# Second feed-forward layer: nine column blocks by seven products, paired PSUM banks, a weight sum on VectorE, whole weight splits

## The chip, the core and the metric

The kernel runs on one core of one Trainium2 chip. The metric is device time in microseconds (us), the median of several executions. TensorE (PE in the profile) multiplies, VectorE (DVE) and ScalarE (ACT) work elementwise, GpSimd (POOL) issues the accumulating DMAs, SyncE (SP) issues the other DMAs. Each engine executes its own instructions in the order in which the built program lists them.

## What is computed

The layer ends in a SwiGLU feed-forward block on 256 tokens of width 2048, and a last normalisation:

```python
def half_step_ffn(x, mod, i, g, w_up, w_down):
    h = adaln(x, g, mod, i)
    a, b = jnp.split(h @ w_up, 2, axis=-1)
    return x + 0.5 * mod[:, i + 2, None, :] * ((jax.nn.silu(a) * b) @ w_down)
...
    xl = half_step_ffn(xl, mod_l, 6, g_norm[l, 2], w_ffn2_up[l], w_ffn2_down[l])
return rms_norm(xl, g_final)
```

`w_up` is 2048 x 11264 and `w_down` 5632 x 2048, in float32. Everything ahead of this second feed-forward block (the first one, attention, the mLSTM heads) is untouched.

## The kernel before

The 5632 hidden columns are 11 blocks of 512, numbered 0 to 10. Block 0 is prepared ahead. For each of the blocks 1 to 10 an **up** step makes the 256 x 512 gated hidden values, which PE transposes (L2052) into `hid2h`/`hid2l`; for each of the blocks 0 to 10 a **down** step multiplies them by 512 rows of `w_down` and adds to `acc2`.

Float32 precision comes from splitting each operand into a high and a low part: `mm3` (L145 to L149) issues three matmuls for each product of a 128 x 128 stationary and a 128 x 512 moving tile. Weights arrive by SP as 128 x 2048 tiles of 1 MB in `raw`, a tile of three buffers. `split` (L117) makes `hi` by ACT (L125) and `lo` by DVE (L126), in two halves of 1024 columns, each in four buffers, so two weight tiles' worth. A `raw` buffer is free again when `hi` and `lo` are made from it; a `hi` or `lo` buffer when PE has read it. These tiles lie in the pool `wp`, which is open for the whole kernel.

An up step comes in two kinds. The **plain** one (`up`, L2151) takes 8 weight tiles and 192 matmuls. The **seven-product** one (`quad`, L2071) regards tokens and inner dimension as 2 x 2 blocks (`a11`, `a12`, `a21`, `a22`) and the weights as 2 x 2 blocks too (first or second half of the inner dimension, gate part a or value part b), and needs seven block products instead of eight: 168 matmuls, with 14 splits of weight tiles, since sums of weight blocks are factors too. Those sums are built in place: `accum` (L728) is a DMA by POOL that adds another weight block to the tile. The table `order` (L2128) gives the seven products in the order `a11, a12, n1, s4, s2, s3, a22`; `n1, s4, s2, s3` are sums of token blocks that `token_forms` makes once. Each product has two weight tiles (q = 0, 1) of 12 matmuls each; X and Y are the PSUM banks that collect them, read by DVE (L2073, L2074) and ACT.

Before the change the blocks 1, 3, 5, 7, 9 go by seven products and 2, 4, 6, 8, 10 by the plain way. A pacing factor, `PACE2`, lays the quads' 70 pieces beside the 73 plain units (an eighth of an up step or a quarter of a down step, one weight tile of 24 matmuls each), so one piece and one unit alternate. Each down unit has its own two PSUM banks, which DVE adds to `acc2` (L2197).

Of the kernel before, what the change touches and what calls it, by code (L numbers as in the profile page):

```python
# [19 lines left out]
P = 128  # L20
# [18 lines left out]
PACE2 = 70 / 73  # L39

# [16 lines left out]
def tile_layer(ctx: ExitStack, tc: tile.TileContext, I: dict, out: bass.AP):  # L57
# [4 lines left out]
    wp = ctx.enter_context(pool(name="wp", bufs=2))  # L62
# [6 lines left out]
    edge.tile([P, 56], F32, name="edge")  # L69

# [46 lines left out]
    def split(raw, n=2048):  # L117

        half = n // 2
# [1806 lines left out]
    with f2x:  # L1926
        def hid_tiles():

            return [f2.tile([P, FB, T], F32R, tag=g, name=g) for g in ("hid2h", "hid2l")]
# [48 lines left out]
        chain_ = [f3.tile([P, 2048], F32, tag=f"c{q}", name=f"chain2{q}") for q in range(2)]  # L1978
# [3 lines left out]
        QUADS = range(1, LAST, 2)  # L1982
# [4 lines left out]
        for q in range(2):  # L1987
            nc.sync.dma_start(chain_[q], part(QUADS[0], 0, q))

# [3 lines left out]
        forms2 = {g: f3.tile([P, 2, 8, P], F32R, tag=f"f{i}", name=f"{g}f") for i, g in enumerate(("n1", "s4", "s2", "s3"))}  # L1993
        n1, s4, s2, s3 = ([x[:, 0], x[:, 1]] for x in (forms2[g] for g in ("n1", "s4", "s2", "s3")))

        def ra_tile():
            return f2b.tile([P, 2048], F32, tag="ra", name="ra")

        def token_forms():
# [3 lines left out]
            f32 = lambda x: [y.bitcast(F32) for y in x]  # L2003

# [16 lines left out]
            v = ra_tile()[:, :1024].rearrange("p (k c) -> p k c", k=8)  # L2021
# [9 lines left out]
            v = ra_tile()[:, :1024].rearrange("p (k c) -> p k c", k=8)  # L2031
# [6 lines left out]
        summed = set()  # L2038

        def turned():  # L2040

            if not turn:
                return
            n, t, sa, sign = turn[0]
            if n >= 2 and n - 2 not in summed or n - 1 not in hids or (n - 1, 0) in [x[:2] for x in turn] or (n - 1, 1) in [x[:2] for x in turn]:
                return
# [17 lines left out]
        def wait_turn(n, t, sa, sign):  # L2064
            turn.append((n, t, sa, sign))
            turn.sort(key=lambda x: x[:2])

# [3 lines left out]
        def quad(n):  # L2071
# [3 lines left out]
            B, ra, g = {}, {}, {}  # L2075
# [17 lines left out]
            def c12():  # L2093
                add(g["b"], B["X"], g["b"])
                mul(g["a"], g["a"], g["b"])
                wait_turn(n, 0, g["a"], -1.0)
# [7 lines left out]
            def c21():  # L2104
# [3 lines left out]
                wait_turn(n, 1, g["a"], -1.0)  # L2108
# [4 lines left out]
            def again(q):  # L2113
                if n + 2 in QUADS:
                    nc.sync.dma_start(chain_[q], part(n + 2, 0, q))

            def loaded(q):
                ra[q] = ra_tile()
                nc.sync.dma_start(ra[q], part(n, 1, 2 + q))
                return ra[q]  # L2120

            def plain(q):
# [4 lines left out]
            held = lambda q: chain_[q]  # L2127
            order = (  # L2128
                (a11, held, "X", True, chained(1, 0), p1),
                (a12, plain, "Y", True, None, c11),  # L2130
                (n1, held, "Y", True, chained(1, 2), kept),
                (s4, loaded, "Y", False, lambda q: accum(ra[q], part(n, 1, q)), p35),
                (s2, held, "X", False, chained(0, 2), c12),
                (s3, lambda q: ra[q], "X", False, None, c22),
                (a22, held, "Y", True, again, c21),
# [15 lines left out]
        def up(n):  # L2151

            sab = []
            for ab in range(2):
                bs = [bank() for _ in range(2)]
                for u in range(4):
# [7 lines left out]
                    if u == 3:  # L2164
                        for t in range(2):
                            if ab:
                                nc.vector.tensor_tensor(sab[t], sab[t], bs[t], op=ALU.mult)
                                wait_turn(n, t, sab[t], 1.0)
# [5 lines left out]
        def block(n, wt, t):  # L2174

            b = bank()
            tt = slice(t * P, (t + 1) * P)
            for j in range(FB):
                w = slice(j * CB, (j + 1) * CB)
                mm3(b, hids[n][0][:, j, tt], hids[n][1][:, j, tt], *wt(w), j == 0, j == FB - 1)  # L2180
            return b

        late = {}

        def down(n):

            assert (n, 1) in done or not n
            for cb in range(NCB):
                wt = load_split(I["w_dn2"][n, cb])
                for t in range(2):  # L2190
# [3 lines left out]
                    if n == 0:  # L2194
                        nc.scalar.activation(a, b, AF.Copy)
                    else:
                        nc.vector.tensor_tensor(a, a, b, op=ALU.add)  # L2197
                    if n == LAST - 1:
                        half_gated(a, a, late["g8"][:, c])
                        accum(a, x2d[t * P : (t + 1) * P, c])  # L2200
# [4 lines left out]
        def units():  # L2205
            yield from up(2)
            yield from down(0)
            for n in (4, 6, 8):
                yield from up(n)
                yield from down(n - 3)  # L2210
                yield from down(n - 2)
            yield from down(7)
            yield from up(10)
            yield from down(8)
# [7 lines left out]
        def quads():  # L2222
            for n in QUADS:
                yield from quad(n)

        forms = token_forms()
        side, n_side, n_quads = quads(), 0, 14 * len(QUADS)
        for u, _ in enumerate(units()):
            steps(forms)
            turned()  # L2230
            while n_side < n_quads and n_side < (u + 1) * PACE2:
                next(side)
                n_side += 1
                turned()
        assert n_side == n_quads
# [159 lines left out]
```

## Time and profile before

| | us |
|---|---|
| median of 3 runs | 2618.13 (2616.05 to 2618.64) |
| profiled execution, first to last instruction | 2616.0 |
| PE busy in it | 2593.1 |
| DVE busy | 2099.3 |
| ACT busy | 1393.4 |
| second feed-forward block on PE, first to last 128 x 512 matmul | 1948.65 to 2606.6 |

The span of the profiled execution is within 0.1 us of the fastest run and 2.1 us under the median. The page gives busy time by engine, then the span in 40 slices, the DMA queues, the chain of work that ended last, and the costliest groups of instructions. A group is a line of the kernel, an engine, an operation, and the tiles it writes and reads. The answers of the trace give the same for a stretch of time, and name what ended an engine's idle time.

### The profile page before, as it was taken

What the parts mean: (1) busy time and instruction counts of PE and PEld (TensorE: products, weight loads), DVE (VectorE), ACT (ScalarE), POOL (GpSimd) and SP (SyncE); (2) the same over time, 40 slices, a digit from 0 to 9 for tenths busy, and PEclk for the clock granted to TensorE, in tenths of its full rate; (3) what the DMA queues carried; (4) which work ended last, traced back from release to release, by engine and by line L of the source; (5) the groups of instructions that cost most, each with busy time, mean ns of one, the idle gap of its engine ahead of it and who ended that gap; (6) DMA issues with size and microseconds to landing.
All of it is one profiled execution on the core that took longest, in us unless ns stands there. A gap on an engine that the chain in (4) does not pass through costs nothing.

```text
span 2616.0 us, 33774 instructions
## 1 busy us (share of the span) xinstructions
PE 2593.1 (99%) x12742; PEld 2159.5 (83%) x12742; DVE 2099.3 (80%) x2792; ACT 1393.4 (53%) x1798; POOL 208.8 (8%) x261
## 2 busy tenths in 40 slices
PE   8999999999999999999999999999999999999998
PEld 5788888888888888888889889878898888888887
DVE  7788888878888788888886889788887676767767
ACT  5455444444444565444454367557576655555554
POOL 0000010100010100000110000220000000000001
PEclk9999999999999999999999999999999999999999
DMA  9889999999999988889986877777769897988875
GB/s 399 347 213 267 281 267 281 256 275 276 277 274 281 265 248 236 226 214 229 230 243 262 311 272 253 240 245 270 248 231 299 261 252 253 253 248 257 242 225 175
DMA packets 126932, 678.93 MB, mean 260 GB/s; under 512 B 14120, under 2 KB 16680, under 8 KB 64944
## 3 DMA queue, kind: packets, MB, share of 16 engines
q1 hardware_dynamic: 99408, 499.54, 51.4%
q0 software_dynamic: 27360, 177.22, 34.9%
q8 instruction: 100, 1.64, 0.2%
q14 instruction: 64, 0.52, 0.1%
HBM read 658.82 MB, written 17.89 MB: 259 GB/s over the span
## 4 chain that ended last, share of the span: by engine, by line
PE 92%; DVE 3%; DMA 3%; issue 1%; ACT 1%; POOL 0%; SPq 0%; ACTq 0%; POOLq 0%; DVEq 0%
PE mm L147 24%; PE mm L149 24%; PE mm L148 24%; PE mm L85 2%; PE tr L148 2%; PE tr L149 2%; PE tr L147 2%; PE Y L149 1%; PE Y L148 1%; PE Y L147 1%; DMA mraw<-in_w_m 1%; PE X L147 1%; PE X L149 1%; PE X L148 1%; PE tr L85 1%; DVE lo L126 1%
## 5 line engine op out<-in xcount | busy, mean ns | idle before, releaser
L125 ACT ACTIVATE hi<-raw 128x1024 fp32r<-128x1024 f32 (+3 forms) x536 | 556.5, 1042 | 579.6 <-PE mm L149 448.8
L126 DVE TENSOR_TENSOR lo<-raw,hi 128x1024 fp32r<-128x1024 f32 (+1 forms) x524 | 630.1, 1208 | 288.2 <-ACT hi L125 268.8
L125 ACT ACTIVATE hi<-chain 128x1024 fp32r<-128x1024 f32 x320 | 338.1, 1060 | 257.3 <-PE mm L149 150.1
L126 DVE TENSOR_TENSOR lo<-chain,hi 128x1024 fp32r<-128x1024 f32 x320 | 386.8, 1221 | 84.4 <-ACT hi L125 80.0
L147 PE MATMUL mm<-hi,hhi 128*128 128x512 f32 (+3 forms) x1024 | 394.6, 385 | 0.0
L148 PE MATMUL mm<-lo,hhi 128*128 128x512 f32 (+3 forms) x1024 | 387.6, 379 | 0.0
L149 PE MATMUL mm<-hi,hlo 128*128 128x512 f32 (+3 forms) x1024 | 387.3, 378 | 0.0
L205 DVE SCALAR_TENSOR_TENSOR junk<-sraw,cBh 128x1024 fp8e5<-128x1024 f32 x192 | 234.4, 1221 | 26.0 <-DMA sraw<-in_w_mt 23.7
L149 PEld LDWEIGHTS mm<-hi,hlo 128*128 128x128 f32 x1024 | 192.9, 188 | 34.0
L147 PEld LDWEIGHTS mm<-hi,hhi 128*128 128x128 f32 x1024 | 192.9, 188 | 31.4
L148 PEld LDWEIGHTS mm<-lo,hhi 128*128 128x128 f32 x1024 | 193.2, 189 | 30.7
L149 PE MATMUL mm<-hi,hid2l 128*128 128x512 f32 x352 | 137.4, 390 | 0.0
L147 PE MATMUL mm<-hi,hid2h 128*128 128x512 f32 x352 | 137.2, 390 | 0.0
L148 PE MATMUL mm<-lo,hid2h 128*128 128x512 f32 x352 | 137.1, 389 | 0.0
L148 PE MATMUL mm<-lo,h2hi 128*128 128x512 f32 x320 | 124.9, 390 | 0.1
L147 PE MATMUL mm<-hi,h2hi 128*128 128x512 f32 x320 | 124.9, 390 | 0.0
L149 PE MATMUL mm<-hi,h2lo 128*128 128x512 f32 x320 | 124.6, 389 | 0.0
L205 DVE SCALAR_TENSOR_TENSOR sr<-sr,cBl 128x1024 f32<-128x1024 f32 x85 | 102.8, 1219 | 14.7 <-DMA sr<-in_w_mt 14.4
L728 POOL DMA_DIRECT2D chain<-in_w_up1b x60 | 53.0, 884 | 725.3 <-DVE lo L126 698.4
L147 PE MATMUL mm<-hhi,hi 128*128 128x512 f32 (+1 forms) x288 | 101.2, 351 | 0.0
L149 PE MATMUL mm<-hhi,lo 128*128 128x512 f32 (+1 forms) x288 | 98.9, 343 | 0.0
L148 PE MATMUL mm<-hlo,hi 128*128 128x512 f32 (+1 forms) x288 | 98.9, 343 | 0.0
(514 smaller groups left out, 5456.3 us busy)
## 6 DMA issues: line engine op xcount, KB each, us to landing
raw<-in_w_dn SPq DMA_DIRECT2D x70, 1024.0 KB, 7.0
chain<-in_w_up1b POOLq DMA_DIRECT2D x60, 1024.0 KB, 10.5
raw<-in_w_up2b SPq DMA_DIRECT2D x50, 1024.0 KB, 5.7
sraw<-in_w_mt SPq DMA_DIRECT2D x96, 512.0 KB, 8.7
sr<-in_w_mt SPq DMA_DIRECT2D x82, 512.0 KB, 5.3
raw<-in_w_up1b SPq DMA_DIRECT2D x40, 1024.0 KB, 8.1
mraw<-in_w_m SPq DMA_DIRECT2D x32, 1024.0 KB, 7.6
chain<-in_w_dn POOLq DMA_DIRECT2D x30, 1024.0 KB, 8.6
```

Source lines behind the costliest of these rows:

```text
L85: ins = getattr(self.engine, name)(*a, **k)
L125: scalar[0].activation(hi, src, AF.Copy)
L126: vector[0].tensor_tensor(lo, src, hi.bitcast(F32), op=ALU.subtract)
L147: tensor[0].matmul(out_ap, sh, mh, start=first, stop=False, skip_group_check=skip)
L148: tensor[0].matmul(out_ap, sh, ml, start=False, stop=False, skip_group_check=skip)
L149: tensor[0].matmul(out_ap, sl, mh, start=False, stop=last, skip_group_check=skip)
L205: ins = nc.vector.scalar_tensor_tensor(junk() if junk else raw, raw, 1.0, cB[s], op0=ALU.mult, op1=ALU.mult, accum_out=mT[:, i, s, kt, h : ...
L728: accum = lambda dst, src: nc.gpsimd.dma_start(dst, src, accum_op=ALU.add)
```

## The change

- Blocks 2 to 10 go by seven products, block 1 alone by the plain way. The order is now fixed: three plain units, then the nine quads one after another, with one plain unit after the products `a12`, `n1`, `s2`, `s3` (in the first quad also after the others).
- The down steps of blocks 1 to 8 go in pairs (`down_pair`): two blocks' products collect in the same two banks, and DVE adds to `acc2` once for both.
- The tile of the third weight block, which was loaded a second time and added by an accumulating DMA, is loaded once and early (`next_third`) and added to the chain by DVE, 128 x 2048, after the split of `n1`'s tile. Two sets of two chain tiles, c and r, change roles from quad to quad.
- `wp` moves to the right side and is closed at the start of this block. Its place goes to `f3`, which now holds the weights: `raw` in **two** buffers, `hi` and `lo` whole (128 x 2048) in **three**. `token_forms` takes one of the two `raw` buffers for its intermediate values, and writes `s3` over `a21`.

```diff
 def raw_tile(n=2048):
+    if wide:
+        return wide["pool"].tile([P, 2048], F32, tag="raw", name="raw", bufs=2)
...
 def split(raw, n=2048):
+    if wide:
+        hi, lo = (wide["pool"].tile([P, 2048], F32R, tag=x, name=x, bufs=3) for x in ("hi", "lo"))
+        nc.scalar.activation(hi, raw, AF.Copy)
+        nc.vector.tensor_tensor(lo, raw, hi.bitcast(F32), op=ALU.subtract)
...
+wcm.__exit__(None, None, None)
 f3 = ctx.enter_context(pool(name="f3", bufs=1, side="right"))
-acc2 = f2.tile([P, 2, D], F32, name="acc2", bufs=1)
+wide["pool"] = f3
+acc2 = f3.tile([P, 2, D], F32, name="acc2")
+sets = [[f3.tile([P, 2048], F32, tag=f"{g}{q}", name=f"chain2{g}{q}") for q in range(2)] for g in "cr"]
-QUADS = range(1, LAST, 2)
+QUADS = range(2, LAST + 1)
 for q in range(2):
-    nc.sync.dma_start(chain_[q], part(QUADS[0], 0, q))
+    nc.sync.dma_start(sets[0][q], part(QUADS[0], 0, q))
+for q in range(2):
+    nc.sync.dma_start(sets[1][q], part(QUADS[0], 1, 2 + q))
...
+        raw = raw_tile()
+        vs = [raw[:, x * 1024 : (x + 1) * 1024].rearrange("p (k c) -> p k c", k=8) for x in range(2)]
...
-    (n1, held, "Y", True, chained(1, 2), kept),
-    (s4, loaded, "Y", False, lambda q: accum(ra[q], part(n, 1, q)), p35),
+    (n1, held, "Y", True, lambda q: add(chain_[q], chain_[q], ra[q]), kept),
+    (s4, third, "Y", False, lambda q: accum(ra[q], part(n, 1, q)), p35),
     (s2, held, "X", False, chained(0, 2), c12),
-    (s3, lambda q: ra[q], "X", False, None, c22),
-    (a22, held, "Y", True, again, c21),
+    (s3, third, "X", False, next_first, c22),
+    (a22, held, "Y", True, next_third, c21),
...
+def down_pair(n):
+    bs = {}
+    for c0 in (0, 2):
+        for m in (n, n + 1):
+            for cb in (c0, c0 + 1):
+                if m == n:
+                    bs[cb] = [bank() for _ in range(2)]
+                wt = load_split(I["w_dn2"][m, cb])
+                for t in range(2):
+                    block(m, wt, t, bs[cb][t], m == n, m > n)
+                if m > n:
+                    for t in range(2):
+                        a = acc2[:, t, cb * CB : (cb + 1) * CB]
+                        nc.vector.tensor_tensor(a, a, bs[cb][t], op=ALU.add)
+                yield
...
+for _ in range(3):
+    unit()
     steps(forms)
+for n in QUADS:
+    behind = {0: 2, 1: 1, 2: 1, 3: 1, 4: 1, 5: 1, 6: 1} if n == QUADS[0] else {1: 1, 2: 1, 4: 1, 5: 1}
+    for step, _ in enumerate(quad(n)):
+        if step % 2:
+            unit(behind.get(step // 2, 0))
+        if n == QUADS[0] and step == 7:
+            drain(forms)
```

How the change moves instructions is shown at two places; the lines of the changed kernel count on by some numbers, L147 there is the load in `load_split` (L140 before), L124 is the whole `lo`, L2081 an addition.

**First place: SP's queue where this block begins.** `raw_15956` and `raw_16015` are the last loads of the part ahead. Before, the first three weight tiles of `up(2)` follow, each in a `raw` buffer that DVE has read, and then the chain's two tiles:

```order
L140 DMA raw_15956<-in_w_up2 128x2048 [waits DMAHW7_49,DMAHW4_49,DVE_49]
L140 DMA raw_16015<-in_w_up2 128x2048 [waits DMAHW5_49,DMAHW0_49,DVE_49]
L140 DMA raw_16110<-in_w_up2b 128x2048 [waits DMAHW6_49,DVE_49]
L140 DMA raw_16172<-in_w_up2b 128x2048 [waits DMAHW7_49,DVE_49]
L140 DMA raw_16233<-in_w_up2b 128x2048 [waits DMAHW0_49,DVE_49]
L1988 DMA chain20_16100<-in_w_up2b 128x2048 [waits DVE_49,PE_49]
```

In the changed program:

```order
L147 DMA raw_15956<-in_w_up2 128x2048 [waits DMAHW7_49,DMAHW4_49,DVE_49]
L147 DMA raw_16015<-in_w_up2 128x2048 [waits DMAHW5_49,DMAHW0_49,DVE_49]
L1997 DMA chain2c0_16101<-in_w_up2b 128x2048 [waits DMAHW0_49,DMASW0_49,DMAHW6_49,DVE_49,DMAHW7_49,PE_49,Activation_49]
L1997 DMA chain2c1_16102<-in_w_up2b 128x2048
L1999 DMA chain2r0_16103<-in_w_up2b 128x2048
L1999 DMA chain2r1_16104<-in_w_up2b 128x2048
L147 DMA raw_16114<-in_w_up2b 128x2048
L147 DMA raw_16150<-in_w_up2b 128x2048 [waits DMAHW5_49,DVE_49]
L147 DMA raw_16184<-in_w_up2b 128x2048 [waits DMAHW6_49,DVE_49]
```

Four chain tiles stand ahead of the first `raw`, and the first of them waits for PE: its wait is for the last matmul of the part ahead, which reads the closed pool's `hi` and `lo`. `raw_16150`, `raw_16184` and the seven `raw` loads after them each wait for the `lo` of the `raw` load just before, since `token_forms` holds the other buffer.

**Second place: DVE and SP around the turn from one quad to the next** (here from block 6 to block 7). DVE before, in a quad: whole tiles in two halves, a `raw` unit and a chain piece in turn:

```order
L126 TENSOR_TENSOR lo_17252<-chain20_16100,hi_17251 128x1024
L2073 TENSOR_TENSOR ca_17097<-Y_17135,ca_17097 128x512
L126 TENSOR_TENSOR lo_17256<-chain20_16100,hi_17255 128x1024
L126 TENSOR_TENSOR lo_17275<-raw_17272,hi_17274 128x1024
L126 TENSOR_TENSOR lo_17279<-raw_17272,hi_17278 128x1024
L126 TENSOR_TENSOR lo_17309<-chain21_16101,hi_17308 128x1024
```

DVE in the changed program (the first two rows are `a11`'s tiles, `raw_18027` and `raw_18045` those of `a12`, `raw_18065` is the down unit behind it, `chain2c0` in the ninth row is `n1`'s first tile):

```order
L124 TENSOR_TENSOR lo_17984<-chain2c0_16101,hi_17983 128x2048
L124 TENSOR_TENSOR lo_18008<-chain2c1_16102,hi_18007 128x2048
L2081 TENSOR_TENSOR ca_17910<-Y_17944,ca_17910 128x512
L124 TENSOR_TENSOR lo_18030<-raw_18027,hi_18029 128x2048
L2082 TENSOR_TENSOR ca_17910<-ca_17910,cy_17728 128x512
L124 TENSOR_TENSOR lo_18048<-raw_18045,hi_18047 128x2048
L2069 SCALAR_TENSOR_TENSOR hid2l_17867<-tr_18000,hid2h_17866 128x4x128
L124 TENSOR_TENSOR lo_18068<-raw_18065,hi_18067 128x2048
L2081 TENSOR_TENSOR ca_18024<-Y_18026,ca_18024 128x512
L124 TENSOR_TENSOR lo_18099<-chain2c0_16101,hi_18098 128x2048
L2219 TENSOR_TENSOR acc2_16100<-acc2_16100,mm_17834 128x512
L2081 TENSOR_TENSOR chain2c0_16101<-chain2c0_16101,chain2r0_16103 128x2048
```

And SP there:

```order
L2132 DMA raw_18045<-in_w_up2b 128x2048 [waits DMAHW7_49,DMAHW3_49,DVE_49]
L2128 DMA chain2r0_16103<-in_w_up2b 128x2048 [waits DMASW4_49,DVE_49]
L2128 DMA chain2r1_16104<-in_w_up2b 128x2048 [waits DMASW5_49,DVE_49]
L147 DMA raw_18065<-in_w_dn2 128x2048 [waits DMAHW0_49,DVE_49]
L147 DMA raw_18136<-in_w_dn2 128x2048 [waits DMAHW3_49,DVE_49]
```

Six weight tiles (`a22`'s, `a11`'s, `a12`'s) now follow each other without a unit between them, and `raw_18065` takes the buffer of `raw_18027`: its load waits for `lo_18030`, two splits ahead of its own.

More of the change, by code (lines that the diff above doesn't have):

```diff
@@ L1927, in hid_tiles @@
         def hid_tiles():
-            return [f2.tile([P, FB, T], F32R, tag=g, name=g) for g in ("hid2h", "hid2l")]
+            return [f2.tile([P, FB, T], F32R, tag=g, name=g, bufs=3) for g in ("hid2h", "hid2l")]
         def sab_tile():
@@ L2095, in c12 @@
                 mul(g["a"], g["a"], g["b"])
-                wait_turn(n, 0, g["a"], -1.0)
+                turn.append((clock[0] + 2, n, 0, g["a"], -1.0))
             def c22():
@@ L2172, in up, with block @@
                     yield
-        def block(n, wt, t):
-            b = bank()
+        def block(n, wt, t, b=None, first=True, last=True):
+            b = b if b is not None else bank()
             tt = slice(t * P, (t + 1) * P)
@@ L2205, in units @@
         def units():
[L2206 to L2214, printed above, removed]
+            yield from up(1)
+            yield from down0()
+            for n in range(1, LAST - 2, 2):
+                yield from down_pair(n)
         def before_final():
```

106 lines of the change are left out of this document (55 added, 51 removed).

## The prediction

> **What bounds the kernel now.** I read the page's busy times first, then the stretch of the second feed-forward block, then who waits in it.
>
> ```profile
> span 2616.0 us, 33774 instructions
> PE 2593.1 (99%) x12742; PEld 2159.5 (83%) x12742; DVE 2099.3 (80%) x2792; ACT 1393.4 (53%) x1798; POOL 208.8 (8%) x261
> ...
> 1948.65:2606.60 657.95, 657.84 (x2939) 543.36 (x2937) 479.95 (x485) 368.79 (x393) 42.42 (x49) 1.00 0.84 248
> ...
> ACT hi L125 <- PE mm L149: 196.8, 135, 3.3
> DVE lo L126 <- ACT hi L125: 159.8, 129, 2.8
> ```
>
> The third row is the block alone: its length, then busy time of PE, weight load, DVE, ACT, POOL, the granted clock (1.00), the DMA engines' share (0.84) and GB/s. PE is busy for 657.84 of 657.95 us, DVE for 480 and ACT for 369. The waits agree: ACT waits for PE to free a `hi` buffer, 196.8 us in all, and DVE waits for ACT. So PE sets the time, and everything that reaches it comes early. A busy PE is not yet a PE at its peak, so I take its rate from two matmuls eleven steps apart:
>
> ```profile
> 2603.67 0.39 PE L147 MATMUL mm<-hi,hid2h 128*128 128x512 f32 x1
> ...
> 2606.16 0.39 PE L149 MATMUL mm<-hi,hid2l 128*128 128x512 f32 x1
> ```
>
> 2.49 us by 11 is 0.2264 us each. The block has 5 x 192 (plain up) + 5 x 168 (quads) + 11 x 96 (down) = 2856 such matmuls, 646.6 us; the rest of 657.9 are the transposes. There is no slack to win but in the number of matmuls.
>
> **What the change removes.** Four plain up steps become quads: 4 x (192 - 168) = 96 matmuls, 96 x 0.2264 = **21.7 us** less on PE. That is the whole gain; all other savings are on engines that PE does not wait for. Paired banks drop 32 of 72 additions of 682 ns from DVE, but DVE gets 178 whole splits for 302 halves and 2 whole ones, 18 weight sums and four more quads' six additions:
>
> ```profile
> L126 DVE TENSOR_TENSOR lo<-raw,hi 128x1024 fp32r<-128x1024 f32 x182 | 221.8, 1223 | 151.7 <-ACT hi L125 150.8
> L126 DVE TENSOR_TENSOR lo<-chain,hi 128x1024 fp32r<-128x1024 f32 x80 | 97.0, 1221 | 8.8 <-ACT hi L125 5.8
> L2197 DVE TENSOR_TENSOR acc<-acc,mm 128x512 f32<-128x512 f32 x72 | 49.1, 682 | 4.7 <-PE mm L149 4.6
> L126 DVE TENSOR_TENSOR lo<-ra,hi 128x1024 fp32r<-128x1024 f32 x40 | 48.7, 1222 | 5.1 <-ACT hi L125 3.2
> L2254 DVE TENSOR_TENSOR lo<-raw,hi 128x2048 fp32r<-128x2048 f32 x2 | 4.6, 2283 | 0.0
> L2253 ACT ACTIVATE hi<-raw 128x2048 fp32r<-128x2048 f32 x2 | 3.8, 1920 | 1.4 <-DMA raw<-in_w_dn 1.4
> ```
>
> 178 x 2.28 = 406 against 372 us now; 18 sums at the price of a whole `lo`, 2.28 (no sum of this shape runs today; its nearest row is the same operation on the same sizes) are 41; 24 additions are 16; 32 fall, 22. DVE rises from 480 to about 545 of some 636 us. On average it still fits, so I charge nothing for DVE's total; where it stands in the way locally comes below. Six accumulating DMAs for each quad instead of eight, on POOL, free DMA time, but four more quads use it up.
>
> **What it adds, first place: the opening.** Today the block's first weights are on the way long before PE wants them:
>
> ```profile
> 1931.56 10.46 SPq L140 DMA_DIRECT2D raw<-in_w_up2b  x3
> ...
> L149 PE MATMUL tr<-h2hi,lo x32: 281/283/283, 1937.5 to 1948.7; 128*128 128x256 f32 x32
> ...
> L147 PE MATMUL mm<-hi,h2hi x320: 388/389/486, 1948.8 to 2536.3; 128*128 128x512 f32 x160
> ```
>
> Three loads start from 1931.6, and PE goes over from the part ahead (last matmul at 1948.7) without a gap. In the changed program SP's first load waits for that last matmul, its end at about 1949, and four chain tiles go ahead of the first `raw`. How fast five loads land, and one alone, and one beside accumulates, three stretches show:
>
> ```profile
> DMA packets 3197, 21.24 MB, mean 425 GB/s; under 512 B 352, under 2 KB 352, under 8 KB 992
> ...
> raw<-in_w_up2b SPq DMA_DIRECT2D x3, 1024.0 KB, 4.8
> ...
> raw<-in_w_dn SPq DMA_DIRECT2D x6, 1024.0 KB, 7.6
> chain<-in_w_up2b POOLq DMA_DIRECT2D x3, 1024.0 KB, 10.5
> ```
>
> The first row is a stretch of plain loads alone (10 to 60 us), the second 2152 to 2186 us, without accumulates, the others 2104 to 2148 us, with them. Five tiles are 5.24 MB: 12.3 us at 425 GB/s, and 2.2 more, since one tile of 2.5 us at that rate takes 4.8. So `raw` lands 14.5 us after PE stopped; `hi` takes 1.92, `lo` 2.28, with handovers 0.2: PE starts in earnest after **18.9 us**.
>
> Then one `raw` buffer serves ten tiles in turn, the eight of `up(1)` and the two of `a12`, as `token_forms` has the other until `s3` is made. From one `lo` to the next is landing + 1.92 + 2.28 + 0.15. By what runs beside them I give six landings 4.8, two 7.6 (accumulates just issued), one 6: 50 us, and 2 us more where four splits and sums of `n1` stand before a unit's `lo` on DVE. Nine cycles are 50 + 2 + 9 x 4.35 = 91 us. PE's own work in that time, eight units of 24 matmuls (5.43 us) and eight quad tiles of 12 (2.72), is 65.2 us and lies beside it. The last unit ends at 18.9 + 91 + 5.0 = 115 us, against 65.6 without waits: **+49 us**. With every landing 4.8 and no wait on DVE it is 41, with every one 7.6 it is 68.
>
> **Second place: each turn of quads.** Eight times (blocks 3 to 10) the down unit behind `a12` waits for its load. Count from PE's start of `a11`, so that `a11` and `a12` keep PE busy until 4 x 2.72 = 10.9. With three `hi` buffers, `a12`'s first `hi` may start when PE ends `a22`, 0.2; it ends at 2.1. DVE makes `a11`'s second `lo` until 1.7, adds for `ca` (0.69) until 2.4, and makes `a12`'s first `lo` until 4.7. Only that frees the `raw` buffer. The load lands 7.6 later, as the two accumulates into `a11`'s tiles were issued just before: 12.4. `hi` until 14.3, `lo` until 16.7. PE can use `hi` alone for two matmuls (0.45). The gap is 16.7 - 10.9 - 0.45 = 5.4 us. With a landing of 4.8 it is 2.6.
>
> What is queued behind: ACT's `hi` of `n1` stands behind that `hi`, and DVE's sum of Y, two additions to `acc2` and a weight sum stand ahead of `n1`'s second `lo`, which then comes 0.9 us late by the same count. That falls beside the slow clock of the next paragraph, and I charge it only in the upper end.
>
> A gap costs more than itself if PE's clock drops. The trace has one case:
>
> ```profile
> 1745.20:1748.60 3.40, 1.14 (x12) 1.11 (x11) 3.40 (x8) 1.89 (x3) 0.00 (x0) 1.00 0.95 336
> 1748.60:1752.00 3.40, 3.40 (x10) 2.72 (x10) 1.27 (x3) 1.76 (x4) 0.00 (x0) 0.50 0.84 283
> ```
>
> In 3.4 us PE was busy for 1.14 (a gap of 2.3 us); in the next 3.4 us it was granted 0.50 of its clock, which loses 1.7 us. A gap of 5.4 leaves PE less busy than that in some such stretch wherever it begins, so I add 1.7: 7.1 a turn, **8 x 7.1 = 57 us**. [...]
>
> **The end.** After the last quad nine down units' loads follow in two buffers, with two more tiles of 1 MB (`g8`, `gf`) ahead of them in SP's queue, and the last four tiles have 2.72 us of PE work each before the next is wanted, against half of 4.8 + 4.35 for a pair of buffers. I take 3.5 us for the load behind `g8` and `gf` and 3.5 for the last tiles: **+7 us**, between 0 and 12.
>
> **The sum.** 2616.0 - 21.7 + 49 + 57 + 7 = 2707 for the profiled execution; the median lies 2.1 above it, so **2709 us**.
>
> **The rivals.**
>
> *The loads are hidden in the turns* (0.12). If `a12`'s first `lo` comes 5 us earlier than I count, only the opening and the end cost: 2616 - 21.7 + 49 + 7 + 2 = 2652. For it speaks that ACT and DVE are idle a good part of the time now; against it that the third `hi` buffer, not an engine, holds that `lo` back.
>
> *The saved matmuls win* (0.04): faster. The mechanism is the same pace as now, PE without gaps, 2618 - 21.7 = 2596. It needs the opening and the eight turns to lose less than 21.7 us together, under 1 us in each turn even if the opening loses only 14. The rows against it are the 12.3 us that five tiles take at 425 GB/s, and the single buffer behind. A result within 0.2% (5 us, about what a measurement of this kernel can tell from no change) would be chance: 0.02.
>
> *The accumulates are late as well* (0.12). `s3`'s tiles are `s4`'s with an accumulate between; from `s4`'s `lo` to `s3`'s `hi` PE has four quad tiles and a unit, 16.3 us, and with 4.2 for `hi` and `lo` some 12 are left for an accumulate of 10.5 that has a second one right behind it. If they miss it, or the sum on DVE shows, each turn costs 4 us more: 2709 + 32 = 2741. For it speaks the DMA share, 0.84 now; a turn of a quad and four units will move 12 + 4 tiles in some 68 us.
>
> The forecast itself has 0.70.
>
> **Range and chances.** Lower end: all landings 4.8, no slow clock, nothing at the end: 2616 - 21.7 + 41 + 8 x 2.6 + 2 = 2658, put at 2655. Upper end: 68 for the opening, 8 x 8 in the turns, 12 at the end, with the 2 of the median 2740, and a little more for accumulates: 2745. It leaves out the faster cases and part of the worst. Faster by over 0.2%: 0.04; within: 0.02; slower: 0.94.
>
> **What would show it.** In the changed profile: PE idle for some 19 us from 1949; then, to about 2064, units that start 9 to 12 us apart, ACT waiting for `raw` by DMA; PE's granted clock at 0.5 in parts of it; from there a gap of 5 us about every 68 us ahead of a down unit, with the wait of `hi` on DMA `raw<-in_w_dn` as its cause. Matmuls of 512 columns fall by 96. DVE's busy time in the block is near 545. If ACT's waits for DMA are small and PE idles on DVE, the splits and sums are the bound and I am wrong in the cause; if units in the opening start 5.4 us apart, both buffers are in use and the order's waits have misled me.

## The result and the profile after

The changed kernel takes **2759.99 us** (median of 4 runs, 2756.28 to 2762.61), the one before 2618.39 us beside it: a ratio of 1.0539, 95% interval 1.0524 to 1.0554. It is slower, as forecast, but by 142 us where I had 91, and 15 us outside the range. Medians here and below are of fast runs alone; one run of the later transposes, of 8511 us, is left out.

The head of the page:

```profile
span 2760.9 us, 33250 instructions
PE 2618.9 (95%) x12646; PEld 2161.0 (78%) x12646; DVE 2165.4 (78%) x2666; ACT 1415.4 (51%) x1686; POOL 221.3 (8%) x275
```

PE issues 96 matmuls fewer (12646 for 12742) and is yet busy for longer: a first sign of a lower clock. Three stretches of the block, in the columns of the prediction's third row (length, busy time of PE, weight load, DVE, ACT, POOL, granted clock, DMA share, GB/s):

```profile
1949.00:2064.00 115.00, 78.40 (x278) 59.14 (x277) 60.61 (x36) 40.38 (x29) 3.58 (x4) 0.78 0.50 161
2064.00:2720.00 656.00, 579.68 (x2451) 465.25 (x2450) 461.33 (x291) 340.61 (x236) 46.99 (x54) 0.94 0.79 228
2720.00:2761.00 41.00, 29.63 (x121) 23.20 (x119) 29.00 (x42) 14.15 (x23) 4.59 (x6) 0.87 0.51 151
```

Before, PE was busy for 657.84 of 657.95 us at clock 1.00. Now it idles in all three stretches, and the clock is below 1.00 in all three; the DMA engines are less busy than before (0.84). The last stretch reaches 10 us past the last matmul of this block (2751.07). So on average no engine is full, and PE waits. For whom, from 2060 us on (engine, line, awaited; us in total, times, longest):

```profile
ACT hi L123 <- DMA raw<-in_w_dn: 85.7, 12, 9.7
PE mm L154 <- ACT hi L123: 50.0, 8, 7.1
...
ACT hi L123 <- DMA chain2c<-in_w_up2b: 23.3, 7, 4.3
ACT hi L123 <- DMA chain2r<-in_w_up2b: 23.3, 7, 4.3
...
PE tr L2064 <- DVE ca L2082: 17.2, 14, 2.6
...
PE mm L155 <- DVE lo L124: 9.8, 9, 1.8
```

Eight times PE waits for a `hi`, 3.9 us at the first turn, 5.8 at the second, 6.5 to 7.1 at the others, and ACT for that `hi`'s load of a down weight: the place that the prediction named. The last row is mostly the short wait for `lo` right behind. Two kinds were not in the forecast's sum: the transposes wait for VectorE's product `ca`, and ACT for accumulated chain tiles. PE's rows at the start, and in the third, fourth and last of the eight turns show sizes:

```profile
1966.37 1.22 PE L154 MATMUL mm<-hi,h2hi 128*128 128x512 f32 x2 [16.71 <-ACT hi L123]
...
2067.60 0.39 PE L156 MATMUL mm<-hi,h2lo 128*128 128x512 f32 x1
...
2265.53 1.22 PE L154 MATMUL mm<-hi,hid2h 128*128 128x512 f32 x2 [6.59 <-ACT hi L123]
...
2339.65 1.22 PE L154 MATMUL mm<-hi,hid2h 128*128 128x512 f32 x2 [6.49 <-ACT hi L123]
2341.97 0.80 PE L155 MATMUL mm<-lo,hid2h 128*128 128x512 f32 x1 [1.10 <-DVE lo L124]
...
2640.89 1.22 PE L154 MATMUL mm<-hi,hid2h 128*128 128x512 f32 x2 [6.88 <-ACT hi L123]
```

Bracketed is PE's idle time before the row. The first row is the opening gap of 16.71 us; the second is the last matmul of `up(1)`, 119 us after 1948.65, where the prediction had 115, against 65.6 without waits. From the third to the last row lie five turns, 75.07 us each. A turn's 264 matmuls are 59.8 us at 0.2264, its two groups of transposes 1.0 (the 11.3 us that the block before spent on its 22 groups): **14.3 us are lost in a turn**, twice the 7.1 of the forecast.

### The profile page after: what moved, and what is told of

Its sections match the earlier page's. It is cut to its first block, busy times and chain, and to the rows that moved or that the text cites. A ratio compares the mean times of both kernels' runs of the same rounds, so it can differ in the third digit from the quotient of the medians.

```text
span 2760.9 us, 33250 instructions
## 1 busy us (share of the span) xinstructions
PE 2618.9 (95%) x12646; PEld 2161.0 (78%) x12646; DVE 2165.4 (78%) x2666; ACT 1415.4 (51%) x1686; POOL 221.3 (8%) x275
## 4 chain that ended last, share of the span: by engine, by line
PE 27%; DMA 10%; DVE 6%; issue 5%; ACT 3%; POOL 0%; SPq 0%; ACTq 0%; POOLq 0%; DVEq 0%
PE mm L155 7%; PE mm L156 7%; PE mm L154 6%; DMA raw<-in_w_dn 3%; DVE lo L124 3%; DMA chain2c<-in_w_up2b 2%; DMA chain2r<-in_w_up2b 2%; ACT hi L123 2%; DMA raw<-in_w_up2b 1%; PE Y L154 1%; PE Y L155 1%; PE Y L156 1%; PE mm L1712 1%; DVE lo L133 0%; PE tr L1529 0%
## 5 line engine op out<-in xcount | busy, mean ns | idle before, releaser
L132 ACT ACTIVATE hi<-raw 128x1024 fp32r<-128x1024 f32 (+3 forms) x352 | 362.3, 1033 | 371.9 <-PE mm L156 257.8
L133 DVE TENSOR_TENSOR lo<-raw,hi 128x1024 fp32r<-128x1024 f32 (+3 forms) x340 | 406.8, 1202 | 139.5 <-ACT hi L132 121.2
L132 ACT ACTIVATE hi<-chain 128x1024 fp32r<-128x1024 f32 x240 | 253.3, 1059 | 234.8 <-PE mm L156 133.5
L133 DVE TENSOR_TENSOR lo<-chain,hi 128x1024 fp32r<-128x1024 f32 x240 | 290.3, 1222 | 81.1 <-ACT hi L132 79.7
L124 DVE TENSOR_TENSOR lo<-raw,hi 128x2048 fp32r<-128x2048 f32 x68 | 155.7, 2290 | 143.6 <-ACT hi L123 143.4
L123 ACT ACTIVATE hi<-raw 128x2048 fp32r<-128x2048 f32 x68 | 130.1, 1913 | 195.4 <-DMA raw<-in_w_dn 85.7
L154 PEld LDWEIGHTS mm<-hi,hhi 128*128 128x128 f32 x1024 | 192.6, 188 | 31.2
L124 DVE TENSOR_TENSOR lo<-chain2c,hi 128x2048 fp32r<-128x2048 f32 x56 | 127.5, 2289 | 36.4 <-ACT hi L123 36.4
L124 DVE TENSOR_TENSOR lo<-chain2r,hi 128x2048 fp32r<-128x2048 f32 x52 | 118.4, 2289 | 34.2 <-ACT hi L123 34.2
L123 ACT ACTIVATE hi<-chain2c 128x2048 fp32r<-128x2048 f32 x56 | 106.6, 1913 | 57.1 <-DMA chain2c<-in_w_up2b 23.3
L123 ACT ACTIVATE hi<-chain2r 128x2048 fp32r<-128x2048 f32 x52 | 99.2, 1914 | 55.8 <-DMA chain2r<-in_w_up2b 23.3
## 6 DMA issues: line engine op xcount, KB each, us to landing
chain<-in_w_up1b POOLq DMA_DIRECT2D x60, 1024.0 KB, 10.2
```

The lines of the kernel that those rows point to most:

```text
L123: nc.scalar.activation(hi, raw, AF.Copy)
L124: nc.vector.tensor_tensor(lo, raw, hi.bitcast(F32), op=ALU.subtract)
L132: scalar[0].activation(hi, src, AF.Copy)
L133: vector[0].tensor_tensor(lo, src, hi.bitcast(F32), op=ALU.subtract)
L154: tensor[0].matmul(out_ap, sh, mh, start=first, stop=False, skip_group_check=skip)
```

## The experiments

My theory after the result: the opening loses 54 us to the released pool, the chain tiles ahead and the single buffer; each turn loses some 14 because the down unit behind `a12` finds no free raw buffer in time, its load then lands late, and the clock falls. Rivals: the DMA engines are the bound of the turns, wherever a load is issued; VectorE is the bound, by whole splits and weight sums. All diffs are against the changed kernel. Times are medians; each kernel's "before" lay between 2617.6 and 2619.3 us.

### Four raw buffers, paid for by half splits

```
-            return wide["pool"].tile([P, 2048], F32, tag="raw", name="raw", bufs=2)
+            return wide["pool"].tile([P, 2048], F32, tag="raw", name="raw", bufs=4)
...
-            hi, lo = (wide["pool"].tile([P, 2048], F32R, tag=x, name=x, bufs=3) for x in ("hi", "lo"))
+            for h in range(2):
+                hi, lo = (wide["pool"].tile([P, 1024], F32R, tag=x, name=x, bufs=4) for x in ("hi", "lo"))
```

> The wide split is made in two halves of 1024 columns (four buffers of 4 KB each for hi and for lo instead of three of 8 KB), and the room pays for four raw buffers instead of two; nothing is left out. Theory (the turns lose to the shortage of raw buffers, and the half clock is only its consequence): the down unit behind a12 has its load issued long ahead, so in each of eight turns the gap of 6.5 us, the gap of 1.1 us behind it and the 5.1 us of half clock go, 8 x 12.7 = 101 us; the opening gets three free buffers instead of one and loses some 25 us less, of 54. Time 2635 us (2610 to 2665). Rival, the DMA engines are the bound (loads land in 11 us beside the accumulating ones, whenever they are issued): at most half of the gap goes, the time stays at 2700 to 2740. Rival, VectorE is the bound (whole splits and the weight sum): two more instructions per tile, no gain, 2755 or more.

Measured: 2630.45 us, 1.0042 of before (1.0027 to 1.0058), 130 us less than the changed kernel and close to the 2635 I expected. Loads of down weights in this run, from 2100 to 2580 us (count, size, median us from issue to landing), and the stretch of the turns:

```profile
raw<-in_w_dn SPq DMA_DIRECT2D x34, 1024.0 KB, 11.4
```

```profile
2030.00:2592.00 562.00, 552.20 (x2437) 449.05 (x2436) 476.74 (x446) 371.81 (x394) 46.17 (x53) 1.00 0.91 264
```

The loads land no sooner, in 11.4 us, but with four buffers they are issued two raw tiles earlier, and ACT's waits for them are gone from this stretch (85.7 us from 2060 us on in the changed kernel): PE is busy for 552 of 562 us at full clock. So the DMA engines, at 0.91 of their time, do not bound the turns as a whole; nor does VectorE, which has more instructions here.

### Half splits with two raw buffers

The same edit with `bufs=2` for raw and `bufs=6` for the halves: the room of the changed kernel.

> The control to the run with four raw buffers: the wide split in halves of 1024 columns, but in six buffers each (the same bytes as three whole ones) and with two raw buffers as in the change. Nothing is left out. Theory (it was the number of raw buffers): the down unit's load still waits for the split of a12's first tile; PE can start on the first half some 1 to 2 us earlier in each turn, and each buffer comes free 0.7 us earlier in the opening, 2740 us (2722 to 2760), gaps of 4 us or more in every turn. Rival (the whole 128x2048 splits were the cost): the time falls near the 2630 us of that run, 2680 at most.

Measured: 2725.82 us, 34 less than the changed kernel; 20 were expected. A turn of it on PE:

```profile
2392.64 0.51 PE L158 MATMUL mm<-hi,hid2h 128*128 128x512 f32 x1 [2.49 <-ACT hi L126]
2393.90 0.79 PE L159 MATMUL mm<-lo,hid2h 128*128 128x512 f32 x1 [0.75 <-DVE lo L127]
```

The gap is smaller than the 4 us I had put as its least, as PE starts on a half, but it stays: 20.3 us of waits for `hi` in all, for 50.0 in the changed kernel, while PE's waits for `ca` rise from 17.2 to 27.0. Of the 34 us, 8 are won in the opening (the last matmul of `up(1)` is at 2059.86, for 2067.60) and the rest behind it. So of the 130 us of the run before, 34 come with the halves and **95 with the two further raw buffers**, though these also take two of six half buffers away.

### The turns: what makes the load late

The two accumulating DMAs behind `a11` left out:

```
-                (a11, held, "X", True, chained(1, 0), p1),
+                (a11, held, "X", True, None, p1),
```

> The change, but without the two accumulating DMAs behind a11 (weights of n1 then lack one summand, so the product is not the reference's; 18 of 54 accumulates are left out, all else stays, also the wait of the down unit's load for the split of a12's first tile). Theory (the gap was 1 to 2 us longer than forecast because that load lands in 11.5 us beside two accumulates): it lands in 5 to 7 us, the gap falls from 6.5 to 1 or 2 us, the half clock from 10.2 us to 3.4 or none, 8 x 8 = 64 us less, 2696 us (2680 to 2720). Rival (the load is late because it is issued late, and lands late beside the other down unit's load): the gap stays over 4 us, 2735 or more.

Measured: 2690.47 us, 70 less (64 expected). In the changed kernel, the issues of the two accumulates and of the load at the turn of 2333, and the `hi` that waits for that load (start, length, engine):

```profile
2321.48 0.86 POOL L735 DMA_DIRECT2D chain2c<-in_w_up2b  x1 [26.72 <-DVE lo L124]
2323.68 0.86 POOL L735 DMA_DIRECT2D chain2c<-in_w_up2b  x1 [1.34 <-DVE lo L124]
...
2326.11 0.33 SPq L147 DMA_DIRECT2D raw<-in_w_dn  x1
...
2337.69 1.91 ACT L123 ACTIVATE hi<-raw 128x2048 fp32r<-128x2048 f32 x1 [9.11 <-DMA raw<-in_w_dn]
```

The load is issued 2.4 us after the second accumulate and lands in 11.5 us. The same load and the next, us to landing, in this run, then PE behind `a12` and the stretch of the turns:

```profile
raw<-in_w_dn SPq DMA_DIRECT2D x2, 1024.0 KB, 4.8
```

```profile
2313.61 0.50 PE L155 MATMUL mm<-lo,hid2h 128*128 128x512 f32 x1 [1.59 <-DVE lo L124]
```

```profile
2064.00:2652.00 588.00, 559.41 (x2452) 451.55 (x2451) 462.24 (x292) 340.04 (x236) 33.05 (x38) 0.99 0.74 227
```

The landing falls from 11.5 to 4.8 us, the gap from 6.5 plus 1.1 to 1.6, and the clock rises from 0.94 to 0.99. The load's wait for a buffer was left as it was. So the late issue alone costs a gap of 1.6 us; the landing behind two accumulates makes the rest. A turn of this run takes 65.3 us (its rows of 2183.49 and 2575.36 lie six turns apart), 4.5 above the work of 60.8, where the changed kernel loses 14.3. PE's waits for `ca` hardly change (13.9 us for 17.2), so they have another cause. This gain and that of more buffers are two cures of one gap; I did not run them together.

### The clock

```
+                    if n >= 3 and step // 2 == 1:
+                        tb = tbank()
+                        for _ in range(28):
+                            nc.tensor.matmul(tb, a11[0][:, 0, :], n1[0][:, 0:4, :].rearrange("p k c -> p (k c)"), ...)
                     unit(behind.get(step // 2, 0))
```

> In each of eight turns 28 matmuls of no use (resident operands, into a spare bank that nobody reads) stand behind a12, 28 x 0.2264 = 6.3 us, as long as the gap; nothing is left out. Theory (the half clock of 10.2 us in each turn is the answer to the gap, and the gap itself is a load that no matmul touches): the gap is filled, the clock stays whole, each turn gains the 5.1 us that half clock costs, 8 x 5.1 = 41 us, time 2720 us (2710 to 2738). Rival, the half clock comes from something else than PE's idle time: the time stays at 2758 or rises by what the added matmuls last beyond the gap, up to 2775.

Measured: 2740.95 us, 19 less, with 224 matmuls more. The clock in the changed kernel around the gap of 2333, and in this run over the turns:

```profile
2330.90:2334.30 3.40, 2.26 (x10) 1.52 (x9) 0.00 (x0) 0.00 (x0) 0.00 (x0) 1.00 0.97 263
2334.30:2337.70 3.40, 0.00 (x0) 0.00 (x0) 0.00 (x0) 0.01 (x1) 0.00 (x0) 1.00 0.99 345
2337.70:2341.10 3.40, 1.22 (x2) 0.50 (x2) 1.47 (x1) 3.40 (x2) 0.00 (x0) 0.50 0.43 183
2341.10:2344.50 3.40, 2.53 (x6) 2.06 (x7) 3.40 (x3) 2.62 (x3) 0.00 (x0) 0.50 0.44 120
2344.50:2347.90 3.40, 3.40 (x9) 2.66 (x9) 1.04 (x3) 0.00 (x0) 0.00 (x0) 0.50 0.47 193
2347.90:2351.30 3.40, 3.40 (x16) 2.78 (x16) 3.29 (x3) 1.18 (x1) 0.00 (x0) 1.00 0.00 0
```

```profile
2064.00:2720.00 656.00, 630.80 (x2766) 513.06 (x2765) 481.85 (x316) 348.88 (x248) 50.25 (x59) 0.99 0.81 234
```

Here PE's idle time did set the clock: with the gap filled it is 0.99, not 0.94. But my 41 us were wrong twice. In the 10.2 us at half clock PE was busy for only 7.15 (1.22 + 2.53 + 3.40), so they cost 3.6 us, not 5.1. And of those 8 x 3.6 = 29 us, 19 came back by the medians (26 between the two profiled executions). The balance is not clean: from 2060 us on PE's waits for `ca` fell from 17.2 to 1.4 us, and those for `lo` rose from 9.8 to 22.2, among them 1.6 us in most turns (1.59 at 2345.75) in the unit behind `n1`, where the changed kernel has none. So the slow clock had covered some waits and made others. The first two rows also show the DMA engines full, 0.97 and 0.99, while the late load is under way, though their average is 0.79.

### The opening

The forms' scratch taken from `acc2`, which frees the second raw buffer:

```
-            raw = raw_tile()
-            vs = [raw[:, x * 1024 : (x + 1) * 1024].rearrange("p (k c) -> p k c", k=8) for x in range(2)]
+            vs = [acc2[:, 0, x * 1024 : (x + 1) * 1024].rearrange("p (k c) -> p k c", k=8) for x in range(2)]
```

> The token forms take their scratch from acc2, which lies idle until the first down unit, instead of one of the two raw buffers; nothing else changes. Theory (the opening loses 54 us, 17 of them at its start to the closed pool and the chain tiles ahead, the rest because one raw buffer serves ten tiles): the units' loads overlap in two buffers, 10 to 30 us less, 2740 us (2728 to 2750); the turns keep their gaps of 6 to 7 us and their half clock. Rival, the opening is bound by what the DMA engines carry (four chain tiles and the units' loads, 10 to 14 us a load): within 5 us of 2760.

The same, and raw, `hi` and `lo` in a pool that waits for no release:

```
+        f3a = f2x.enter_context(pool(name="f3a", bufs=1))
-        wide["pool"] = f3
+        wide["pool"] = f3a
...
-        forms2 = {g: f3.tile([P, 2, 8, P], F32R, tag=f"f{i}", name=f"{g}f") for i, g in enumerate(("n1", "s4", "s2"))}
+        forms2 = {g: (f3 if i == 2 else f3a).tile([P, 2, 8, P], F32R, tag=f"f{i}", name=f"{g}f") for i, g in enumerate(("n1", "s4", "s2"))}
```

> Raw, hi, lo and two of the token forms lie in a pool on the left side, in room that is free before the split buffers of the part ahead are released; chain tiles, acc2 and the third form lie where those were; the forms' scratch is acc2. So the block's first units wait neither for the release nor behind four chain tiles, and have two raw buffers. Nothing is left out, and the turns are as they were. Theory: PE's gap of 16.7 us at the start goes, and most of the other 37 us of the opening: 40 us less, 2720 us (2708 to 2738). Rival, the opening is held by the landing of the loads as such: the gap moves into the first unit, 2740 to 2760.

Measured: 2728.31 us (32 less) and 2720.35 us (40 less). The first stretches of the two runs:

```profile
1949.00:2032.00 83.00, 60.34 (x257) 48.35 (x255) 55.93 (x34) 36.69 (x26) 3.58 (x4) 0.88 0.66 220
```

```profile
1949.00:2030.00 81.00, 70.90 (x278) 55.79 (x277) 57.97 (x35) 38.93 (x27) 3.59 (x4) 0.87 0.68 222
```

Both lie in the ranges I gave. The last matmul of `up(1)` is at 2040.84 and 2035.86, for 2067.60 in the changed kernel: the single buffer was worth 27 of the opening's 54 us, the early pool 5 more, and the rest of the 32 and 40 us comes behind the opening. The early pool takes the gap of 16.7 us at the start away and gives so little, because with two buffers PE then waits in later units, at a clock that is still 0.87.

### Parts of the change undone

The weight sum of `n1` by accumulating DMA instead of VectorE, and each down block in its own bank:

```
-                (n1, held, "Y", True, lambda q: add(chain_[q], chain_[q], ra[q]), kept),
+                (n1, held, "Y", True, chained(1, 2), kept),
```

> One part of the change undone: the sum of n1's weights is again made by two accumulating DMAs from HBM, not by VectorE from the tile that lies in SBUF. Nothing is left out. Theory (what bounds the turns is room and the DMA engines, not VectorE): two more accumulates of 1 MB in each of nine quads, those behind s4 and s2 land later, s3's and a22's weights are waited for 2 to 4 us longer, 2785 us (2768 to 2815). Rival (VectorE is the bound in the turns): its 2 x 2.3 us per quad go, 2735 to 2755.

```
-                            block(m, wt, t, bs[cb][t], m == n, m > n)
-                        if m > n:
-                            for t in range(2):
-                                a = acc2[:, t, cb * CB : (cb + 1) * CB]
-                                nc.vector.tensor_tensor(a, a, bs[cb][t], op=ALU.add)
+                            a = acc2[:, t, cb * CB : (cb + 1) * CB]
+                            nc.vector.tensor_tensor(a, a, block(m, wt, t), op=ALU.add)
```

> Another part undone: each down block is added into acc2 by itself, not two in one PSUM bank; order, loads and splits stay. Nothing is left out. Theory: 32 more additions of 0.69 us on VectorE, which mostly lie beside PE, and some ahead of a lo that PE waits for: 2763 us (2756 to 2775). Rival (shared banks hold PE back, as the next pair waits for them): 2745 to 2755.

Measured: 2742.32 us, 18 **less** with VectorE's sums undone, and 2758.93 us, no difference, with the banks undone (2763 expected). My theory of the first was wrong in sign; the time is in the rival's range. Of PE's waits (from 2060 us), the row that differs most from the changed kernel's above:

```profile
PE tr L2064 <- DVE ca L2082: 5.5, 9, 1.8
```

The wait of the transposes falls from 17.2 to 5.5 us. What the sums do to it can be followed in the changed kernel behind the gap of 2333, on three engines:

```profile
2355.08 2.29 DVE L2081 TENSOR_TENSOR chain2c<-chain2c,chain2r 128x2048 f32<-128x2048 f32 x1
2357.28 4.49 DVE L124 TENSOR_TENSOR lo<-chain2r,hi 128x2048 fp32r<-128x2048 f32 x2
...
2362.18 0.87 POOL L735 DMA_DIRECT2D chain2r<-in_w_up2b  x1 [1.32 <-DVE lo L124]
...
2374.11 1.92 ACT L123 ACTIVATE hi<-chain2r 128x2048 fp32r<-128x2048 f32 x1 [3.07 <-DMA chain2r<-in_w_up2b]
...
2376.06 2.29 DVE L124 TENSOR_TENSOR lo<-chain2r,hi 128x2048 fp32r<-128x2048 f32 x1 [2.10 <-ACT hi L123]
2378.26 0.69 DVE L2082 TENSOR_TENSOR ca<-ca 128x512 f32<-128x512 f32 x1
```

The second sum stands ahead of the `lo` of `s4`'s two tiles; the accumulate into the second tile waits for that `lo`, so `s3`'s `hi` is 3.07 us late, `lo` behind it, and `ca` behind that `lo`; the transposes waited 1.86 us for it, at 2379.10. VectorE itself idles for 2.10 us in this chain. Counted from PE's first row behind the gap, these two accumulates are issued after 20.3 and 22.5 us here, and after 17.1 and 20.3 without the sums. ACT's waits for accumulated tiles fall from 46.6 to 30.6 us in all. So VectorE is no bound by its total; its sums delay the issue of accumulates.

The transposes due two steps later:

```
-                turn.append((clock[0] + 2, n, 0, g["a"], -1.0))
+                turn.append((clock[0] + 4, n, 0, g["a"], -1.0))
```

> The turns of the products' tiles (transposes) are due four steps of the clock after their product instead of two, so they stand on PE behind the first tile of the next product; nothing else changes. Theory (some 2 us in each turn are PE waiting for VectorE's last multiply, which sits behind a lo that an accumulating DMA made late): the waits of PE for ca go, 8 x 2 = 16 us, 2744 us (2736 to 2754). Rival (the time only moves to the tile behind, whose weights are late as well): within 5 us of 2760.

Measured: 2748.98 us, 11 less, where the theory had 16. PE's wait for `ca` is gone, but ACT waits longer for the accumulated tiles (23.3 + 23.3 us in the changed kernel):

```profile
ACT hi L123 <- DMA chain2r<-in_w_up2b: 31.0, 11, 5.2
ACT hi L123 <- DMA chain2c<-in_w_up2b: 26.8, 7, 5.7
```

### Together

Four raw buffers with halves, the early pool, `acc2` as scratch, and the third product's first tiles loaded behind the first three units:

```
-        for q in range(2):
-            nc.sync.dma_start(sets[1][q], part(QUADS[0], 1, 2 + q))
...
             unit()
             steps(forms)
+        for q in range(2):
+            nc.sync.dma_start(sets[1][q], part(QUADS[0], 1, 2 + q))
```

> Halves with four raw buffers, the left-side pool that needs no release, acc2 as the forms' scratch, and the two tiles of the third product loaded behind the first three units instead of ahead of them. Nothing is left out. Theory: of the run with four raw buffers the 15.9 us gap at the block's start go to 2 or 3; the turns lose 2 to 3 us each as there. 2630 - 13 = 2617 us (2608 to 2626), that is, the 96 matmuls fewer only just pay for what is left. Rival (chain tiles and units' loads now collide, 6 MB within 20 us): the first quad waits for its chain tiles, 2626 to 2640.

The same room as three raw and five half buffers of `hi` and `lo` each:

> As the run with all three together, but three raw buffers and five half buffers each of hi and lo (the same room). Theory (what is left of 2 to 3 us a turn is weights that accumulating DMAs bring late, and a split that may run further ahead hides part of it): 2612 us (2604 to 2622), faster than with four raw buffers by about 5. Rival (three raw buffers are one too few for the two loads of a12 and the down unit behind it): gaps of 1 to 3 us behind a12, 2625 to 2650.

Measured: 2613.68 us, 0.9987 of before (0.9977 to 0.9997), where I had 2617, and 2620.12 us, 1.0011 (1.0002 to 1.0020). One raw buffer fewer for one half buffer more of `hi` and `lo` costs 6 us, where I expected a gain of 5: splits that may run further ahead did not pay for the lost buffer, though the loss is less than the rival's.

Then all four measures: besides, the other first chain tiles also behind the three units, the forms begun a unit later, and the later transposes; and the same without the later transposes.

```
-        for _ in range(3):
+        for u in range(3):
             unit()
-            steps(forms)
+            if u:
+                steps(forms)
+        for q in range(2):
+            nc.sync.dma_start(sets[0][q], part(QUADS[0], 0, q))
```

> As the run with four raw buffers and the early pool, and besides: all four first chain tiles are loaded behind the first three units, the token forms begin a unit later, and the turns of the products' tiles are due four steps later. Nothing is left out. Theory (of the 28 us that PE still loses there, 5 are at the opening for the third unit's lo, and 0.5 to 0.8 in each turn for the transposes): 2604 us (2597 to 2611), 0.5% faster than the kernel before. Rival (as in the run with later transposes alone, the time comes back in the next tile): 2611 to 2618.

> The version with all four measures, but the transposes due two steps after their product again, as in the change. Nothing is left out. Theory (each of seven turns lost 0.5 to 0.8 us to them with four raw buffers): 2614 us (2611 to 2618), 4 us more. Rival (what the later transposes give, the next tile takes): 2608 to 2611.

Measured: **2610.39 us, 0.9969 (0.9956 to 0.9981)** and 2609.36 us, 0.9967 (0.9955 to 0.9979), where I had 2604 and 2614: both lie 0.3% below the kernel before, clear of noise but small, and 5% below the changed kernel. The later transposes give nothing where there is room, as the rival said. Last, the sums by DMA in the version with all four:

> The version with all four measures, but the sum of n1's weights again by two accumulating DMAs. Nothing is left out. Theory (VectorE's sum cost 18 us in the tight version because it pushed splits back that PE was waiting for; with room the splits run ahead, and VectorE has 90 us of slack in 658): nothing to gain, and 18 accumulates more while the DMA engines are 88% busy: 2614 us (2608 to 2630). Rival (the sum is a cost of its own): 2595 to 2605.

Measured: 2633.50 us, 23 **more** than with VectorE's sums, and above both forecasts. The turns of the version with VectorE's sums, then of this one, and its waits:

```profile
2011.00:2569.00 558.00, 553.77 (x2460) 452.80 (x2459) 479.29 (x451) 373.76 (x398) 46.99 (x54) 1.00 0.92 269
```

```profile
2011.00:2590.00 579.00, 559.90 (x2426) 450.50 (x2425) 434.97 (x426) 365.05 (x394) 58.58 (x68) 0.99 1.01 285
```

```profile
ACT hi L126 <- DMA chain2c<-in_w_up2b: 51.9, 20, 4.0
ACT hi L126 <- DMA chain2r<-in_w_up2b: 51.7, 20, 4.6
```

With PE running free, the eighteen added accumulates fill the DMA engines (1.01 for 0.92), and ACT waits for chain tiles 40 times, 103.6 us in all, for 14 times and 42.2 us with VectorE's sums. So the weight sum by VectorE paid in the version whose DMA engines were nearly full (0.92), and cost in the one where they had room (0.79).

## Why the prediction was off

| term | forecast | measured |
|---|---|---|
| 96 matmuls fewer | -21.7 | -21.7 |
| opening | +49 | +53.6 |
| turns | +57 | +109 |
| end | +7 | +4 |
| sum on 2616.0 | +91 | +145 |

Both columns are for profiled executions; that of the changed kernel was 2.6 us above its median. The measured opening is 119.2 - 65.6 from the row of 2067.60. The end is 119 matmuls from 2719.88 to 2751.07, 31.2 us for 26.9. The turns are what is left of 144.9, and agree with 8 x 14.3 = 114, since the first two gaps are shorter.

- **Right:** the direction, the place, and of the cause the scarce raw buffer and the load behind it. PE idles from 1949 (16.7 us for 18.9); the down unit behind `a12` waits in eight turns for a raw buffer and its load; DVE is busy for 551 us in the block (the forecast says about 545; its own terms add up to 549), and is not the bound by its total. The opening's single buffer is confirmed by the 27 us that a second one gave there.
- **The step that failed is the turn: 7.1 us in the sum, 14.3 measured.** It was too low by 2.2 us in the gap, 1.9 in the clock, 2.2 in the wait for `ca`, and 0.9 that I did not follow up.
- **The gap, "The load lands 7.6 later".** It landed in 11.5, as the rows of 2321 to 2338 show. I took the median of six loads over 44 us of the old order; this one is issued 2.4 and 4.6 us after two accumulates, and the run without those two shows 4.8. The gap became 6.5 and 1.1 us, not 5.4. That 3.9 us of landing made it only 2.2 longer has a second cause, which hid part of the error: `a12` ended 12.6 us after `a11`'s first matmul (2320.59), not 10.9, since transposes and short waits stand between, and the two early matmuls took 1.22 us at half clock, not 0.45.
- **The clock, "I add 1.7", was 3.6.** I priced one stretch of 3.4 us. By the rows of 2334 to 2351 the half clock lasted for three, behind one with PE busy for 0.00 us: PE was busy for 1.22, 2.53 and 3.40 of 3.40 in them, so the clock came back when the first that PE filled had ended. In the prediction's two rows of before, the stretch with PE busy for 1.14 of 3.40 had been enough for the fall, and PE filled the very next one (3.40 of 3.40 at 0.50). I had not asked when the clock comes back, and that is what made the price double. What the clock goes by, beyond these rows, was not shown.
- **What I put at nothing:** PE's wait for `ca`, 17.2 / 8 = 2.2 us a turn. It is the mechanism of my rival "the accumulates are late as well", which had 4 us a turn: `s3`'s second `hi` starts 11.9 us after the accumulate's issue, by the rows of 2355 to 2378, and waits. It came on top of the forecast, at half that price. By terms, gap, clock, `ca` and rest: 7.6 + 3.6 + 2.2 + 0.9 = 14.3. The terms are not independent: with the gap filled, the waits for `ca` went as well.
- **Range:** the upper end had 8 us for a turn, made from landings of 7.6 and one stretch of slow clock. Its bound was a median of rows; the landing of a single load right behind two accumulates was in none of them.

Open: why the two accumulates hold the load back that long was not measured by itself; the DMA engines' share was 0.97 and 0.99 at that time, and whether anything else adds to it was not shown. The released pool and the four chain tiles ahead were not tested apart, nor is it known where the opening loses the 22 us that are left with the early pool.

## What to carry to other kernels

When a change makes a buffer scarce, a load's issue moves, and its landing must be priced at the place where it now stands, behind the transfers issued just ahead (11.5 us here), not by a median of loads elsewhere (7.6). A gap on PE cost more than itself here: behind 6.5 us of idle time the clock stood at 0.50 for 10.2 us, by my estimate 3.6 us more. At an average share of 0.79 the DMA engines were still at 0.97 and 0.99 just where a load was awaited. Whether to move work from DMA to VectorE depends on which of them is late at that place, and on what waits for VectorE there, accumulates too: the same edit gave 23 us with more raw buffers and cost 18 without.

## What the runs showed of the hardware

- A plain load of 1 MB landed in 4.8 us with no accumulate ahead of it, in 11.5 when issued 2.4 us behind the second of two accumulates, and in 11.4 in the median beside accumulates in the run with four raw buffers.
- The DMA engines' share was 1.01 at 285 GB/s with eight accumulates for each quad (the version with all four measures and the sums by DMA), while the stretch of plain loads in the prediction moved 425 GB/s.
- In the changed kernel at 2337.7, behind a stretch of 3.4 us with PE busy for 0.00, the granted clock was 0.50 for 10.2 us, until the first stretch that PE filled (3.40 of 3.40) had ended; in the run without two accumulates, where the gap is 1.59 us, the turns had 0.99 on average.
